# Weights of the first FFN staged as f32 and cast by GpSimd, x^T made on TensorE, weights of the last FFN pre-cast: an 8-core decoder trunk on Trainium2

## Chip, cores, metric

The kernel runs on all 8 cores of one Trainium2 chip (two dies: cores 0 to 3 and 4 to 7). Every core does the same work on two of the 16 sequences, with no traffic between cores. The metric is device microseconds of the slowest core.

Some executions fall in a slow state: the cores of one die or both show a lower granted TensorE clock and the time is some per cent longer. Only fast executions enter a ratio. On the chips of this study the slow state was so frequent (kernel before: 5813 to 6769 us) that I use three measures, and name which one I quote:

- the **ratio** to the kernel before of the same rounds, fast executions only, with its 95% interval;
- the **die difference**: over all executions of a kernel, I take every die whose mean granted clock was above 0.968, average the spans of its four cores, and subtract the same mean for the kernel before on the same chip in the same rounds. "±" is twice the standard error over such dies. Moving the threshold to 0.965 moved the differences by about 2 us, apart from the two slowest kernels, which then count more dies and read 8 to 10 us longer;
- the **delay curve**, from the one profiled (fast) execution: the time at which a given share of all matmul columns has started, averaged over the 8 cores, minus the same of the kernel before. It compares single executions, so its end value carries some ±10 us, but its steps over a short stretch carry much less.

## The reference, cut

```python
D_MODEL, BATCH, SEQ, D_FF = 1024, 16, 2048, 2816
def _swiglu(x, w_gate_up, w_down):
    gate, up = jnp.split(x @ w_gate_up, 2, axis=-1)
    return (jax.nn.silu(gate) * up) @ w_down
# layer 0: half FFN -> HGRN2 gated recurrence -> half FFN -> shared K/V
# layer 1: half FFN -> forgetting attention ("FoX") -> half FFN
for l in range(2):
    x = _layer_norm(alpha * x + 0.5 * _swiglu(x, w_gate_up[l, 0], w_down[l, 0]), ...)
    y = _hgrn2(x, ...) if l == 0 else _fox(x, k, v, c, ...)
    x = _layer_norm(alpha * x + y, ...)
    x = _layer_norm(alpha * x + 0.5 * _swiglu(x, w_gate_up[l, 1], w_down[l, 1]), ...)
    # after layer 0: k, v, c = _shared_kv(x, ...)
```

There are four FFN halves, numbered f = 0 to 3. All weights arrive as f32; the kernel multiplies in bf16.

## The kernel before: the parts that matter

Every operation is first *recorded* with a modelled cost and its dependences. A list scheduler then plays the program through a simple model in time, and the order it finds is what each engine's instruction queue gets. On the chip each engine works through its queue in that order (e1 below shows VectorE stand still behind a waiting instruction). So the model of a DMA transfer decides the order of instructions.

```python
def shared(work, overlap):
    overlap = max(0.0, overlap)
    return 2 * work if overlap >= 2 * work else work + overlap / 2

def list_schedule(ops, key):
    ...
        if o.dma is not None:
            if e == "pool":                              # GpSimd: the software queue
                st = max(t + cost + 1.0, sw_free)
                sw_free = o.end = st + shared(o.nbytes / 135e3, dma_free - st)
                o.end += 1.5
            else:                                        # SyncE: the hardware queue
                st = max(t + cost + 1.0, dma_free)
                dma_free = o.end = st + shared(o.nbytes / 300e3, sw_free - st)
                o.end += 1.0
    ...
```

Weights are cast f32 to bf16 by the DMA itself the first time they are used (this has to be issued from GpSimd: the Trainium skill, "DMA: Bandwidth & Descriptors", section "Rules for kernel authors"; all casting transfers are issued there). The bf16 copy is written back to DRAM, and later uses read it over the hardware queue:

```python
    def wload(self, th, key, dst, bufs, chan, scr, src, nb):
        R = self.R
        wb = self.wsb.get(key)
        if wb is None:
            wb = self.wsb[key] = Buf()
            R.dma("pool", [(dst, src)], reads=[self.gate] if th else [], writes=bufs, chan=chan, nbytes=nb)
            R.dma("sp", [(scr, dst)], reads=bufs, writes=[wb], chan=self.wch.next(), nbytes=nb)
        else:
            R.dma("sp", [(dst, scr)], reads=[wb], writes=bufs, chan=chan, nbytes=nb)
```

The two sequences are cut into 8 blocks of 512 rows, and the stages are recorded in a hand-written order: `p` the first FFN of blocks 0 and 1 together, `a` that of another block alone, `h` HGRN2, `c` the FFN after it, `k` K/V, `d` the third FFN, `x` attention, `e` the last FFN, `i` the load of a block's x^T.

```python
    def record(self):
        ...
        self.xin(0, *blk[0])        # x^T of a block: 1 MB as bf16, by a casting transfer
        self.xin(1, *blk[1])
        ...
        head = "p0 i2 h0 a2 h1 h2 c0 k0 d0 x0 c1 k1 d1 x1 c2 k2 d2 e0 x2 i3 a3 e1 h3 i4 a4"
    ...
    def ffn(self, blocks, f):
        ...
        for half in range(2):
            for jj in range(HJ):
                j = half * HJ + jj
                w = self.wg.next()
                self.wload(0, ("gu", f, j), w.t[:], [w.b], w.b, self.wgu_s[f, j], self.wgu_f[f, j], 1 << 19)
                if jj in (1, 3, 5):
                    ...                                        # one third of this half's w_down
                    self.wload(0, ("dn", f, half, g), ...)
                ...                                            # gate, up, tanh, two multiplies
            for (n, s, b), (hT, hTb, rD, banks, lt) in work:
                ...                                            # down projection, residual, layer norm
```

The softmax here doesn't subtract the row's maximum and nothing guards it: scores larger than these inputs give would overflow.

## Time and profile before

| | before |
|---|---|
| four executions | 5829.5, 5834.3, 5836.6, 6063.0 (slow) us, median 5835.4 |
| cores of the profiled execution | 5777.0 to 5848.9 us, mean 5815.1, mean granted clock 0.972 to 0.977 |
| PE (TensorE) busy, slowest core | 5478.3 us |

In the profile PE is TensorE, PEld its weight loads, DVE VectorE, ACT ScalarE, POOL GpSimd and SP SyncE; a q after a name marks what the engine's sequencer does, such as issuing a transfer. A buffer is written `out<-in`.

Lines of the profile's page of the kernel before. The first gives the span; then PE's busy time (its share of the span and the instructions); then, for 40 equal slices of the span, PE's busy share and the mean of the 16 DMA engines in tenths; last, the chain of waits by engine.

```profile
span 5848.9 us, 77661 instructions; the slowest of 8 cores (5777.0 to 5848.9 us)
...
PE 5478.3 (94%) x31296; PEld 2603.6 (45%) x31296; DVE 3056.6 (52%) x5516; ACT 2129.0 (36%) x4154; POOL 273.8 (5%) x410
...
PE   6988989899997999999999999999999999989998
...
DMA  9678897965669864656566374664656556455454
...
PE 81%; DMA 11%; DVE 3%; ACT 2%; issue 2%; SPq 1%; POOL 0%; DVEq 0%; POOLq 0%; ACTq 0%
```

PE is the limit. What can be gained is its 370 us of idle time, most of it in the first third. The change aims at two stretches: the first slice, and slices 13 and 14 (1755 to 2047 us), where DMA stands at 9 and 8.

What PE waited for in the first 250 us of the kernel before (line, what it waited for: us in total, times, longest):

```profile
core 6 of [0, 1, 2, 3, 4, 5, 6, 7], span 5848.9 us
...
PE pb L650 <- DMA wg_6<-w_gu: 36.7, 2, 25.6
PE pb L650 <- DMA wg_10<-w_gu: 9.0, 1, 9.0
PE pb L650 <- DMA wg_8<-w_gu: 7.6, 2, 6.1
```

And between 1650 and 2020 us, where the last FFN's first pass (`e0`) runs beside an attention block (`x2`):

```profile
core 6 of [0, 1, 2, 3, 4, 5, 6, 7], span 5848.9 us
...
PE pb L1108 <- DMA fka_2_72<-ka_d: 30.1, 3, 22.8
PE pb L1108 <- DMA fka_2_73<-ka_d: 10.0, 1, 10.0
...
```

`fka` are the attention's keys. They come late because f32 weights (`w_gu`, `w_dn` of f = 3) fill the DMA engines. The busy times of both stretches on core 6 (window: its length, then busy us of PE, PEld, DVE, ACT, POOL, the granted clock, DMA share, GB/s):

```profile
0.00:110.00 110.00, 58.12 (x224) 23.91 (x224) 26.02 (x65) 9.85 (x16) 11.46 (x28) 0.86 1.00 214
...
1740.00:1990.00 250.00, 204.21 (x1364) 102.35 (x1363) 85.12 (x149) 90.04 (x179) 19.71 (x34) 0.90 0.85 202
...
```

PE idles 52 us in the first, 46 us in the second. And the DMA queues in the first 250 us (queue: packets, MB, share of the 16 engines' time):

```profile
q0 software_dynamic: 6944, 22.58, 58.5%
q1 hardware_dynamic: 8920, 25.96, 32.0%
...
```

Software transfers took 58.5% of the engines' time for 22.58 MB: 0.585 x 250 / 22.58 = 6.5 us per MB. Hardware ones took 3.1.

### The profile page before, as it was taken

To read this page: it belongs to the slowest core of one execution; us is meant where nothing else is said; L and a number is where in the kernel's file an instruction comes from. 1 tells how busy PE (TensorE), PEld (TensorE's weight loads), DVE (VectorE), ACT (ScalarE), POOL (GpSimd) and SP (SyncE) were. 2 spreads that over 40 slices of the span, in tenths; PEclk is the share of its full clock that TensorE was granted. 3 is DMA by queue.
4 is the path that set the end of the run, shared out by engine and by line. 5 is a ranking of instruction groups with operands and counts; after the bars stand their busy time and mean duration, and the time that the engine had idled before them with its cause. 6 is when DMAs were issued, how large, how long until landed. Compare 5 with 4: busy or idle time off the path is not lost.

```text
span 5848.9 us, 77661 instructions; the slowest of 8 cores (5777.0 to 5848.9 us)
## 1 busy us (share of the span) xinstructions
PE 5478.3 (94%) x31296; PEld 2603.6 (45%) x31296; DVE 3056.6 (52%) x5516; ACT 2129.0 (36%) x4154; POOL 273.8 (5%) x410
## 2 busy tenths in 40 slices
PE   6988989899997999999999999999999999989998
PEld 2443434444543444444454445444454444544544
DVE  2466656554543546667454653556535565244255
ACT  1153535221313315253331525325253351742720
POOL 1001111000000000000000000000000000000000
PEclk8999989999998999999999999999999999999999
DMA  9678897965669864656566374664656556455454
GB/s 216 164 202 219 199 240 178 250 200 177 185 195 214 220 207 131 203 175 211 185 179 213 118 233 159 208 198 140 202 174 196 183 180 204 159 189 187 141 175 155
DMA packets 383494, 1106.28 MB, mean 189 GB/s; under 512 B 66784, under 2 KB 80800, under 8 KB 370592
## 3 DMA queue, kind: packets, MB, share of 16 engines
q1 hardware_dynamic: 353840, 1004.80, 53.8%
q0 software_dynamic: 29296, 96.51, 10.4%
q8 instruction: 248, 4.06, 0.3%
q14 instruction: 110, 0.90, 0.1%
HBM read 989.54 MB, written 208.14 MB: 205 GB/s over the span
## 4 chain that ended last, share of the span: by engine, by line
PE 81%; DMA 11%; DVE 3%; ACT 2%; issue 2%; SPq 1%; POOL 0%; DVEq 0%; POOLq 0%; ACTq 0%
PE pb L650 70%; PE pb L1108 4%; PE pb L1124 2%; DMA ka_d<-hT 2%; DMA lw_38<-hqf_s 1%; DMA wg_9<-wgu_s 1%; PE pb L697 1%; PE pb L961 1%; DMA fka_2_72<-ka_d 1%; DMA wg_6<-w_gu 1%; DMA v_d<-hT 1%; SPq L244 1%; DMA wg_7<-wgu_s 1%; PE pb L940 1%; PE pb L957 1%
## 5 line engine op out<-in xcount | busy, mean ns | idle before, releaser
L650 PE MATMUL pb<-wd,hT 128*128 128x512 bf16 x5456 | 1247.5, 380 | 12.5 <-DVE rD_15 L762 5.3
L650 PEld LDWEIGHTS pb<-wd,hT 128*128 128x128 bf16 x5456 | 523.2, 98 | 613.9 <-DVE hT L738 8.8
L732 ACT ACTIVATE sg_14<-pb 128x512 f32<-128x512 f32 x352 | 210.0, 597 | 920.5 <-PE pb L650 917.7
L732 ACT ACTIVATE sg_13<-pb 128x512 f32<-128x512 f32 x352 | 209.9, 596 | 892.5 <-PE pb L650 891.1
L735 DVE SCALAR_TENSOR_TENSOR sg_14<-sg_14,pb 128x512 f32<-128x512 f32 x352 | 241.3, 685 | 553.9 <-ACT sg_14 L732 553.4
L735 DVE SCALAR_TENSOR_TENSOR sg_13<-sg_13,pb 128x512 f32<-128x512 f32 x352 | 241.2, 685 | 460.7 <-ACT sg_13 L732 459.8
L738 DVE SCALAR_TENSOR_TENSOR hT<-sg_14,pb 128x512 bf16<-128x512 f32 x352 | 241.0, 685 | 175.2 <-PE pb L650 158.1
L738 DVE SCALAR_TENSOR_TENSOR hT<-sg_13,pb 128x512 bf16<-128x512 f32 x330 | 225.7, 684 | 161.1 <-PE pb L650 146.9
L650 PE MATMUL pb<-xT_3,wg_6 128*128 128x512 bf16 x880 | 212.7, 389 | 38.6 <-DMA wg_6<-w_gu 36.7
L650 PE MATMUL pb<-xT_3,wg_10 128*128 128x512 bf16 x880 | 209.8, 387 | 19.8 <-DMA wg_10<-w_gu 9.0
L650 PE MATMUL pb<-xT_3,wg_8 128*128 128x512 bf16 x896 | 214.7, 386 | 14.4 <-DMA wg_8<-w_gu 7.6
L650 PE MATMUL pb<-xT_4,wg_10 128*128 128x512 bf16 x912 | 214.9, 381 | 9.0 <-DVE hT L992 7.1
L650 PE MATMUL pb<-xT_3,wg_7 128*128 128x512 bf16 x880 | 210.0, 385 | 6.0 <-DMA wg_7<-wgu_s 4.1
L650 PE MATMUL pb<-xT_4,wg_9 128*128 128x512 bf16 x848 | 200.4, 382 | 13.9 <-DMA wg_9<-wgu_s 6.4
L650 PE MATMUL pb<-xT_4,wg_6 128*128 128x512 bf16 x912 | 213.3, 382 | 0.0
L650 PE MATMUL pb<-xT_4,wg_8 128*128 128x512 bf16 x880 | 206.4, 381 | 7.1 <-DMA wg_8<-wgu_s 3.5
L650 PE MATMUL pb<-xT_3,wg_9 128*128 128x512 bf16 x880 | 203.9, 379 | 0.3 <-DMA wg_9<-wgu_s 0.2
L650 PE MATMUL pb<-xT_4,wg_7 128*128 128x512 bf16 x864 | 200.9, 379 | 2.4 <-DVE hT L992 1.2
L650 PE MATMUL pb<-xT_5,wg_9 128*128 128x512 bf16 x592 | 141.9, 384 | 13.9 <-DMA wg_9<-wgu_s 10.0
L650 PE MATMUL pb<-xT_5,wg_7 128*128 128x512 bf16 x608 | 146.6, 385 | 6.2 <-DMA wg_7<-wgu_s 3.3
L1117 ACT ACTIVATE fPT_2_76<-pb 128x512 bf16<-128x512 f32 (+1 forms) x216 | 122.9, 569 | 71.0 <-PE pb L1108 44.1
L650 PEld LDWEIGHTS pb<-xT_3,wg_6 128*128 128x128 bf16 x880 | 85.6, 100 | 140.9 <-issue 34.4
(507 smaller groups left out, 9307.5 us busy)
## 6 DMA issues: line engine op xcount, KB each, us to landing
wd<-wdn_s SPq DMA_DIRECT2D x108, 1024.0 KB, 7.4
wg_9<-wgu_s SPq DMA_DIRECT2D x120, 512.0 KB, 4.4
wg_10<-wgu_s SPq DMA_DIRECT2D x120, 512.0 KB, 4.8
wg_8<-wgu_s SPq DMA_DIRECT2D x119, 512.0 KB, 4.8
wg_7<-wgu_s SPq DMA_DIRECT2D x118, 512.0 KB, 4.8
wg_6<-wgu_s SPq DMA_DIRECT2D x117, 512.0 KB, 4.7
wd<-wdn_s SPq DMA_DIRECT2D x54, 768.0 KB, 10.3
wd<-w_dn POOLq DMA_DIRECT2D x16, 1024.0 KB, 14.4
```

Of the source, the lines that this page charges most:

```text
L244: ins = eng.dma_start(out=dst, in_=src)
L650: ins = e.matmul(out, lhsT=pairs[i][0], rhs=pairs[i][1], start=(start and i == 0), stop=(stop and i == n - 1))
L697: ins = e.transpose(qv[:, k, :], xb.t[:, k * 128:(k + 1) * 128], self.ident.t[:])
L732: R.op("act", lambda e, sg=sg, pg=pg: e.activation(out=sg.t[:], in_=pg.t[:], func=AF.Tanh, scale=0.5), reads=[pg.b], writes=[sg.b], cost=c ...
L735: R.op("dve", lambda e, sg=sg, pg=pg: e.scalar_tensor_tensor(out=sg.t[:], in0=sg.t[:], scalar=1.0, in1=pg.t[:], op0=ALU.add, op1=ALU.mult) ...
L738: R.op("dve", lambda e, sg=sg, pu=pu, jj=jj, hT=hT: e.scalar_tensor_tensor(out=hT[:, jj, :], in0=sg.t[:], scalar=0.25, in1=pu.t[:], op0=AL ...
L940: ins = e.matmul(Uv[:, x, :], lhsT=bt.t[:, t, :], rhs=V.t[:, t, hv], start=True, stop=True)
L957: R.op("pe", lambda e, t=t, pov=pov, pt=pt, hv=hv: e.matmul(pov[:, t, :], lhsT=pt.t[:, t, :], rhs=V.t[:, t, hv], start=(t == 0), stop=Fals ...
L961: R.op("pe", lambda e, t=t, cc=cc, c=c, pov=pov, A=A, sp=sp: e.matmul(pov[cc * 64:(cc + 1) * 64, t, :], lhsT=A.t[:, c * 64:(c + 1) * 64], ...
L1108: first = ins = e.matmul(ps.t[:, c0:512], lhsT=ka.t[:, i * 128:(i + 1) * 128], rhs=qa.t[:, h4, c0:512], start=True, stop=(i < 4 * b))
L1117: R.op("act", lambda e, ps=ps, pt=pt, c0=c0: e.activation(out=pt.t[:, c0:512], in_=ps.t[:, c0:512], func=AF.Exp), reads=[ps.b], writes=[pt ...
L1124: ins = e.matmul(accv[:, t, 0:65], lhsT=pt.t[:, t * 128:(t + 1) * 128], rhs=Vt.t[:, i, vo:vo + 65], start=(i == 0 and t == 0), stop=(i == ...
```

## The change

The intent: at the start, take the casting load off the software queue (f32 over the hardware queue into two staging buffers, GpSimd casts), and do not load x^T of the first two blocks but make it on TensorE from x, which is needed anyway. Later, convert the last FFN's weights DRAM to DRAM ahead of need, while other stages run, so that `e0` only loads bf16. With this comes a new DMA model in the scheduler: other rates, and transfers that slow each other on both queues.

The diff, cut to its core:

```diff
-def shared(work, overlap): ...
 def list_schedule(ops, key):
         if o.dma is not None:
-            if e == "pool":
-                st = max(t + cost + 1.0, sw_free)
-                sw_free = o.end = st + shared(o.nbytes / 135e3, dma_free - st)
-                o.end += 1.5
-            else:
-                st = max(t + cost + 1.0, dma_free)
-                dma_free = o.end = st + shared(o.nbytes / 300e3, sw_free - st)
-                o.end += 1.0
+            work = o.nbytes / (140e3 if e == "pool" else 325e3)
+            mine, other = (sw_free, hw_free) if e == "pool" else (hw_free, sw_free)
+            st = max(t + cost + 1.0, mine)
+            both = min(work, max(0.0, other - st))
+            mine, other = st + work + both, other + both
+            sw_free, hw_free = (mine, other) if e == "pool" else (other, mine)
+            o.end = mine + 1.5
...
 def wload(...):
-        if wb is None:
+        if wb is None and self.staged:                  # only the first FFN of blocks 0 and 1
+            ... for d, c in parts:
+                st = self.lw.next()                     # one of two staging buffers, seen as f32
+                R.dma("sp", [(f, c)], writes=[st.b], chan=st.b, nbytes=n * 512)
+                R.op("pool", lambda e, d=d, f=f: e.tensor_copy(out=d, in_=f), reads=[st.b], writes=bufs, ...)
+            R.dma("sp", [(scr, dst)], reads=bufs, writes=[wb], chan=self.wch.next(), nbytes=nb)
+        elif wb is None:
...
+    def precast(self, key, gate):                       # DRAM f32 -> DRAM bf16, all on one channel
+        ...
+        self.R.dma("pool", [(scr, src)], reads=[gate], writes=[wb], chan=self.cch, nbytes=nb * 1.3)
...
 def record(self):
-        self.xin(0, *blk[0])
-        self.xin(1, *blk[1])
+        pre = {"d1": gu(3, 0, 6), "c2": gu(3, 6, 16), "d2": gu(3, 16, 22) + dn(3)}
...
+    def xin_pe(self, n, s, b, rD, banks, lt):           # x -> bf16 (VectorE) -> 8 transposes (PE) -> xT (ScalarE)
...
 def ffn(self, blocks, f):
+                for _ in range(due):                    # pre-casts spread over the steps of d1, c2, d2
+                    key = self.pq.pop(0)
+                    if key: self.precast(key, step[0])
```

"All on one channel" means that every pre-cast waits for the one before it to land.

More of the change, by code (lines that the diff above doesn't have):

```diff
@@ L103, in dma @@
         return o
-def shared(work, overlap):
-    overlap = max(0.0, overlap)
-    return 2 * work if overlap >= 2 * work else work + overlap / 2
 def list_schedule(ops, key):
@@ L124, in list_schedule @@
     avail = {e: [] for e in engs}
-    dma_free = sw_free = 0.0
+    hw_free = sw_free = 0.0
     tset = None
@@ L387, in build @@
         self.gate = Buf()
+        self.cch = Buf()
+        self.staged = False
+        self.pq = []
         self.wch = Ring([Buf() for _ in range(8)])
@@ L591, in wload @@
         wb = self.wsb.get(key)
-        if wb is None:
+        if wb is None and self.staged:
+            wb = self.wsb[key] = Buf()
+            parts = [(dst, src)] if key[0] == "gu" else [(dst[:, k:min(k + 2, dst.shape[1])], src[:, k:min(k + 2, dst.shape[1])])
+                                                         for k in range(0, dst.shape[1], 2)]
+            for d, c in parts:
+                st = self.lw.next()
+                n = int(np.prod(d.shape[1:]))
+                f = st.t[:].bitcast(F32)[:, 0:n]
+                if len(d.shape) == 3:
+                    f = f.rearrange("p (k c) -> p k c", c=d.shape[2])
+                R.dma("sp", [(f, c)], writes=[st.b], chan=st.b, nbytes=n * 512)
+                R.op("pool", lambda e, d=d, f=f: e.tensor_copy(out=d, in_=f), reads=[st.b], writes=bufs,
+                     cost=0.2 + n / 960.0)
+            R.dma("sp", [(scr, dst)], reads=bufs, writes=[wb], chan=self.wch.next(), nbytes=nb)
+        elif wb is None:
             wb = self.wsb[key] = Buf()
@@ L597, in wload @@
             R.dma("sp", [(dst, scr)], reads=[wb], writes=bufs, chan=chan, nbytes=nb)
+    def precast(self, key, gate):
+        if key[0] == "gu":
+            scr, src, nb = self.wgu_s[key[1:]], self.wgu_f[key[1:]], 1 << 19
+        else:
+            f, half, g = key[1:]
+            k0, nk = WD_GROUPS[g]
+            rows = slice((half * HJ + k0) * 128, (half * HJ + k0 + nk) * 128)
+            scr, src, nb = self.wdn_s[f, rows], self.wdn_f[f, rows], nk << 18
+        wb = self.wsb[key] = Buf()
+        self.R.dma("pool", [(scr, src)], reads=[gate], writes=[wb], chan=self.cch, nbytes=nb * 1.3)
     def record(self):
@@ L613, in record @@
         tail = "c6 k6 d6 h7 x6 c7 k7 d7 e5 e6 x7 e7"
+        gu = lambda f, a, b: [("gu", f, j) for j in range(a, b)]
+        dn = lambda f: [("dn", f, half, g) for half in range(2) for g in range(3)]
+        pre = {"d1": gu(3, 0, 6), "c2": gu(3, 6, 16), "d2": gu(3, 16, 22) + dn(3)}
         for tok in (head + " " + rest + " " + tail).split():
@@ L626, in record @@
             elif tok[0] == "p":
+                self.pq = pre.get(tok, [])
                 self.ffn([(m,) + blk[m] for m in (n, n + 1)], 0)
             else:
+                self.pq = pre.get(tok, [])
                 self.ffn([(n,) + blk[n]], names[tok[0]])
@@ L634, in xin, with flip, tr @@
                    nbytes=1 << 20)
+    def xin_pe(self, n, s, b, rD, banks, lt):
+        R = self.R
+        for t in range(4):
+            r, xb, q = rD[t], self.xb[lt].next(), banks.next()
+            R.dma("sp", [(r.t[:], self.x_d[s, (b * 4 + t) * 128:(b * 4 + t + 1) * 128, :])], writes=[r.b], chan=r.b,
+                  nbytes=1 << 19)
+            R.op("dve", lambda e, r=r, xb=xb: e.tensor_copy(out=xb.t[:], in_=r.t[:]), reads=[r.b], writes=[xb.b],
+                 cost=c_dve(1024))
+            self.flip(xb, q, n % 3, t, "act")
+    def flip(self, xb, q, slot, t, eng):
+        R = self.R
+        qv = q.t[:].bitcast(BF16).rearrange("p (k c) -> p k c", k=8)
+        def tr(e):
+            first = None
+            for k in range(8):
+                ins = e.transpose(qv[:, k, :], xb.t[:, k * 128:(k + 1) * 128], self.ident.t[:])
+                first = first or ins
+            return (first, ins)
+        R.op("pe", tr, reads=[xb.b, self.ident.b], writes=[q.b], cost=8 * c_pe(128))
+        dst = self.xT[slot][:, :, t * 128:(t + 1) * 128]
+        if eng == "act":
+            R.op("act", lambda e: e.activation(out=dst, in_=qv, func=AF.Copy), reads=[q.b],
+                 writes=[self.xTb[slot][t]], cost=c_act(1024))
+        else:
+            R.op("dve", lambda e: e.tensor_copy(out=dst, in_=qv), reads=[q.b], writes=[self.xTb[slot][t]],
+                 cost=c_dve(1024, 0, 2))
     def mm(self, th, bank, out, pairs, reads, split=4, start=True, stop=True, extra_w=()):
@@ L689, in layer_norm @@
              cost=c_act(1024))
-        tl_ = tg % 4
-        q = bank_ring.next()
-        qv = q.t[:].bitcast(BF16).rearrange("p (k c) -> p k c", k=8)
-        def tr(e):
-            first = None
-            for k in range(8):
-                ins = e.transpose(qv[:, k, :], xb.t[:, k * 128:(k + 1) * 128], self.ident.t[:])
-                first = first or ins
-            return (first, ins)
-        R.op("pe", tr, reads=[xb.b, self.ident.b], writes=[q.b], cost=8 * c_pe(128))
-        R.op("dve", lambda e: e.tensor_copy(out=self.xT[slot][:, :, tl_ * 128:(tl_ + 1) * 128], in_=qv),
-             reads=[q.b], writes=[self.xTb[slot][tl_]], cost=c_dve(1024, 0, 2))
+        self.flip(xb, bank_ring.next(), slot, tg % 4, "dve")
     def ffn(self, blocks, f):
@@ L711, in ffn @@
                  (self.a["phT"][0].t, self.phTb, self.a["prD"], self.bQK, 1)]
+        npq = list(self.pq)
+        self.staged = len(blocks) > 1
         work = list(zip(blocks, homes[::-1][-len(blocks):]))
+        if self.staged:
+            for (n, s, b), (hT, hTb, rD, banks, lt) in work:
+                self.xin_pe(n, s, b, rD, banks, lt)
         for half in range(2):
@@ L725, in ffn @@
                 wv = w.t[:].rearrange("p (k g c) -> p k g c", k=8, g=2)
+                due = len(npq) * (j + 1) // NJ - len(npq) * j // NJ
+                step = [Buf()] if due else []
                 for (n, s, b), (hT, hTb, rD, banks, lt) in work:
@@ L739, in ffn @@
                         out=hT[:, jj, :], in0=sg.t[:], scalar=0.25, in1=pu.t[:], op0=ALU.mult, op1=ALU.mult),
-                        reads=[sg.b, pu.b], writes=[hTb[jj]] + ([self.gate] if len(blocks) > 1 and j == 15 else []),
+                        reads=[sg.b, pu.b], writes=[hTb[jj]] + step + ([self.gate] if len(blocks) > 1 and j == 15 else []),
                         cost=c_dve(512))
+                for _ in range(due):
+                    key = self.pq.pop(0)
+                    if key:
+                        self.precast(key, step[0])
             for (n, s, b), (hT, hTb, rD, banks, lt) in work:
@@ L745, in ffn @@
                     r = rD[t]
-                    if half == 0:
+                    if half == 0 and not self.staged:
                         rows = slice(tg * 128, (tg + 1) * 128)
@@ L766, in ffn @@
                         self.layer_norm(lt, r, s, tg, n % 3, f == 3, banks)
+        self.staged = False
     def out_proj(self, n, s, b, w_s, w_f, scale):
```

## The prediction

> **What bounds it now.** The matrix engine: PE is busy 5478 of 5849 us (engine table); the chain of waits is 81% PE, 11% DMA. The change can touch two pieces of the 370 idle us.
>
> *Start.* In the stretch table PE works 58 of the first 110 us: 52 idle, DMA engines at 97-108%, PE waiting for `wg<-w_gu` (25.6 us to the first matmul, 28 us more after).
>
> *First pass of the last FFN, beside an attention block (1780-1960 us).* DMA is saturated again while f32 weights come on the software queue; PE idles 45 us, 40 of them waiting for `fka<-ka_d` (once 22.8 us).
>
> **Costs.** By the DMA queues of the first 250 us, software took 58.5% of the engines' time for 22.6 MB landed, hardware 32.0% for 26.0 MB: estimates of 6.5 and 3.1 us per MB. A gate-up weight is 0.52 MB as bf16, so 3.4 us by software; 1.05 MB as f32, so 3.2 us by hardware. Moving the queue saves almost no engine time. That agrees with the Trainium skill, "DMA: Bandwidth & Descriptors", section "Issuing engines are not separate DMA queues". Removed at the start: loading x^T for two blocks: 2 x 1.05 MB x 6.5 = 14 us of DMA time.
>
> Added: 64 transposes (8 took 0.6 us), 8 VectorE casts, 8 ScalarE copies, all before PE has work; 33 GpSimd casts of up to 128x2048. The skill, "GPSIMD Engine Reference", section "Engine selection", calls one-input work roughly line rate; I estimate 2-2.5 us each. But they lie in a latency chain: two staging buffers, each doing load, land, cast, and every reload queues behind a bf16 write-back. All of x (4.2 MB) and the layer-norm rows now precede the first weight.
>
> Hand estimate: first FFN matmul at 30-35 us; then a staged chunk every 4.8-5.5 us. Down weights are interleaved early, so the third, fifth and seventh gate-up tiles come late: 15-25 us of stalls, 0-7 us more after the first down projection. Idle 47-65 us against 52: expected loss 6 us.
>
> Pre-casting: the last FFN's 34.6 MB of f32 are converted DRAM to DRAM, one transfer at a time, in 1100-1750 us (DMA share 0.6-0.75). It adds 112 us of engine time there (17.3 MB x 6.5): share 0.8-0.9. In 1740-1990 us it removes the same 112 us; the bf16 write-back is replaced by a bf16 load. DMA share there falls from 85% to near half. Gain 35 of the 40 us. Cost: 10 us of new attention waits in 1100-1750, or layer norms held up behind a blocked GpSimd queue.
>
> **Sum.** 35 - 10 - 6 = 19 us gained: 5815 us, 80% range 5775-5862. The schedule is recomputed with other DMA rates, so small waits everywhere move: +-15 us. Faster by over 2%: 0.04; within 2%: 0.93; slower by over 2%: 0.03.
>
> **What would show it.** PE idle in the first 110 us still 45-65, first FFN matmul after 28 us, PE waits naming GpSimd casts. Cast mean 2-2.5 us. `fka<-ka_d` waits over 10 us gone from the stretch of the last FFN's first pass, PE idle there under 12 us. DMA share 0.8-0.9 in 1100-1750, with some more idle. PE busy total within 10 us of before.
>
> **What would make it wrong.** Casts at 4 us or more (start loses 20 us); f32 by hardware faster than 3.1 us per MB once software is off the rings (start gains 15); pre-casts blocking GpSimd's in-order queue so that layer norms stall PE for tens of us; the reordering hurting an attention stage.

## The result, and the profile after

| | before | after |
|---|---|---|
| executions, us | 5829.5, 5834.3, 5836.6, 6063.0 (slow) | 5876.7, 5898.1, 5908.3, 6023.9 (slow) |
| median, us | 5835.4 | 5903.2 |
| ratio of fast runs | | 1.0101, 95% interval 1.0064 to 1.0138 |
| mean of the 8 cores in the profile | 5815.1 us | 5864.4 us (+49) |
| mean granted clock of the 8 cores | 0.975 | 0.974 |

The ratio counts a fifth execution of the kernel after as well (5886.0 us, fast). A ratio is the mean time of one kernel's fast runs over that of the other's of the same rounds, so it is not quite the ratio of the medians quoted. The change made the kernel 1% slower. That is inside the 2% which counts as the same, but outside its own noise, and outside the predicted range (5775 to 5862 us).

The page of the kernel after, the same parts:

```profile
span 5897.1 us, 77865 instructions; the slowest of 8 cores (5821.7 to 5897.1 us)
...
PE 5502.8 (93%) x31360; PEld 2613.7 (44%) x31360; DVE 3064.0 (52%) x5524; ACT 2140.4 (36%) x4162; POOL 315.1 (5%) x414
...
PE 81%; DMA 10%; DVE 3%; ACT 3%; issue 1%; SPq 1%; POOL 1%; POOLq 0%; DVEq 0%; ACTq 0%
```

PE's waits in the first 250 us of the kernel after:

```profile
core 1 of [0, 1, 2, 3, 4, 5, 6, 7], span 5897.1 us
...
PE pb L680 <- DVE xbL L668: 20.9, 3, 19.2
PE pb L706 <- POOL wg_8 L599: 16.3, 2, 9.8
PE pb L706 <- POOL wg_7 L599: 4.5, 2, 4.2
PE pb L706 <- POOL wg_10 L599: 4.4, 1, 4.4
...
```

The 19.2 us are the wait for the first block of x (the transposes begin at 19.17 us). After that PE waits for GpSimd's casts. Between 1700 and 2100 us PE's longest wait in the kernel after is now another:

```profile
core 1 of [0, 1, 2, 3, 4, 5, 6, 7], span 5897.1 us
...
PE pb L706 <- DMA wg_7<-wgu_s: 20.1, 2, 15.2
...
```

`wgu_s` are the bf16 weights that the pre-casts write. The load that PE waits for 15.2 us was issued at 1862.55 us, when their last pre-cast had long been issued (1775.38) but those of `w_dn` were still running (the last was issued at 1868.92). The same windows of the kernel after, on its slowest core (core 1):

```profile
0.00:110.00 110.00, 63.66 (x275) 29.11 (x276) 30.03 (x72) 17.31 (x23) 28.06 (x27) 0.89 0.92 270
...
1740.00:1990.00 250.00, 225.97 (x1452) 111.37 (x1451) 89.08 (x151) 87.75 (x176) 8.48 (x15) 0.96 0.75 188
...
```

On these two cores both target stretches got better: PE idles 46 us instead of 52 in the first and 24 instead of 46 in the second. The mean of the 8 cores confirms the second (41.6 us before, 24.8 after) but hardly the first (52.0 and 50.4 in the first 110 us, 57.1 and 58.2 in the first 300). Yet the kernel is slower, so the loss lies elsewhere. The mean PE idle time of the 8 cores, worked out from both traces (us):

| stretch, us | before | after |
|---|---|---|
| 0 to 100 | 51.4 | 45.0 |
| 100 to 300 | 5.7 | 13.2 |
| 600 to 1000 | 46.6 | 77.2 |
| 1400 to 1800 | 21.4 | 35.7 |
| 1800 to 2000 | 38.6 | 21.0 |
| 0 to 5600 | 341 | 369 |

Between 600 and 1000 us 31 us are lost, in a stretch (HGRN2 beside FFN) where the change adds no instruction at all. 28 of the 49 us are idle time; the rest is PE busy time. Of that rest, 8 us are the transposes (8 groups of 1.03 us in the trace); part of the other goes with the lower granted clock (see "PE busy total" below).

What PE waited for from 650 to 1150 us, first in the kernel before (lines of VectorE's products alone):

```profile
core 6 of [0, 1, 2, 3, 4, 5, 6, 7], span 5848.9 us
...
PE pb L650 <- DVE sg_13 L735: 2.5, 2, 1.7
...
PE pb L902 <- DVE hB_2_52 L894: 2.2, 3, 1.2
...
PE pb L650 <- DVE sg_14 L735: 0.8, 1, 0.8
...
```

and in the kernel after:

```profile
core 1 of [0, 1, 2, 3, 4, 5, 6, 7], span 5897.1 us
...
PE pb L958 <- DVE hB_2_52 L950: 13.6, 5, 6.8
...
PE pb L706 <- DVE sg_14 L786: 6.7, 4, 4.3
PE pb L706 <- DVE sg_13 L786: 6.5, 4, 3.7
...
```

`hB` is a product of HGRN2 and `sg` the gate of the FFN; VectorE makes both, and PE waits longer for them.

### The profile page after: what moved, and what is told of

Its sections match the earlier page's. It is cut to its first block, busy times and chain, and to the rows that moved or that the text cites. A ratio compares the mean times of both kernels' runs of the same rounds, so it can differ in the third digit from the quotient of the medians.

```text
span 5897.1 us, 77865 instructions; the slowest of 8 cores (5821.7 to 5897.1 us)
## 1 busy us (share of the span) xinstructions
PE 5502.8 (93%) x31360; PEld 2613.7 (44%) x31360; DVE 3064.0 (52%) x5524; ACT 2140.4 (36%) x4162; POOL 315.1 (5%) x414
## 4 chain that ended last, share of the span: by engine, by line
PE 81%; DMA 10%; DVE 3%; ACT 3%; issue 1%; SPq 1%; POOL 1%; POOLq 0%; DVEq 0%; ACTq 0%
PE pb L706 70%; PE pb L1164 4%; DMA lw_38<-hqf_s 3%; PE pb L1180 2%; DMA wg_8<-wgu_s 1%; PE pb L680 1%; PE pb L1017 1%; DMA ka_d<-hT 1%; DMA wg_10<-wgu_s 1%; SPq L237 1%; PE pb L996 1%; DMA lw_39<-w_dn 1%; PE pb L1013 1%; DMA xr_d<-rL_19 1%; DMA fka_2_72<-ka_d 1%
## 5 line engine op out<-in xcount | busy, mean ns | idle before, releaser
L706 PE MATMUL pb<-xT_3,wg_7 128*128 128x512 bf16 x880 | 213.3, 391 | 28.2 <-DMA wg_7<-wgu_s 20.1
L706 PE MATMUL pb<-xT_3,wg_8 128*128 128x512 bf16 x896 | 213.6, 385 | 20.5 <-POOL wg_8 L599 16.3
L706 PE MATMUL pb<-xT_3,wg_10 128*128 128x512 bf16 x880 | 211.6, 388 | 16.2 <-DVE sg_14 L786 4.8
L706 PE MATMUL pb<-xT_4,wg_10 128*128 128x512 bf16 x912 | 214.6, 381 | 9.7 <-DMA wg_10<-wgu_s 4.7
L706 PE MATMUL pb<-xT_4,wg_6 128*128 128x512 bf16 x912 | 213.2, 380 | 3.6 <-DVE sg_14 L786 2.0
L706 PE MATMUL pb<-xT_3,wg_9 128*128 128x512 bf16 x880 | 210.2, 386 | 4.8 <-DMA wg_9<-wgu_s 4.8
L706 PE MATMUL pb<-xT_3,wg_6 128*128 128x512 bf16 x880 | 207.5, 384 | 7.0 <-DVE sg_13 L786 3.7
L706 PE MATMUL pb<-xT_4,wg_8 128*128 128x512 bf16 x880 | 206.0, 380 | 6.0 <-DMA wg_8<-wgu_s 3.4
L706 PE MATMUL pb<-xT_4,wg_9 128*128 128x512 bf16 x848 | 197.2, 379 | 8.6 <-DMA wg_9<-kk_s 2.1
L706 PE MATMUL pb<-xT_4,wg_7 128*128 128x512 bf16 x864 | 200.9, 379 | 4.0 <-ACT hT L1045 1.8
L706 PE MATMUL pb<-xT_5,wg_7 128*128 128x512 bf16 x608 | 143.9, 379 | 4.8 <-DVE sg_13 L786 2.7
L706 PE MATMUL pb<-xT_5,wg_10 128*128 128x512 bf16 x576 | 136.5, 382 | 9.6 <-ACT hT L1045 7.7
L706 PE MATMUL pb<-xT_5,wg_9 128*128 128x512 bf16 x592 | 141.0, 384 | 4.0 <-DMA wg_9<-wgu_s 1.4
```

What stands on the lines that cost most here:

```text
L706: ins = e.matmul(out, lhsT=pairs[i][0], rhs=pairs[i][1], start=(start and i == 0), stop=(stop and i == n - 1))
```

## The experiments

The questions in order: which part of the change costs the time (e1 to e4)? If it is the scheduler's DMA model, is it the size of its rates, its rule, or chance (e5, e6, e7, e9 to e14, e18)? What are the start and the pre-casts worth by themselves (e2, e3, e8, e15, e16, e17)?

Three theories of the model's cost run through the texts. A1: its nominal rates are too high, so consumers are placed too early. A2: chance; any other order is some tens of us worse than one that was tuned by trial. A3: the model tells the scheduler of later data, so it defers work, and an in-order engine then stands still behind an instruction that waits.

All 18 kernels gave correct results. The delay curve of all, as **steps** from one share of the matmul columns to the next (us against the kernel before, where 10% is reached at 671 us, 16% at 1072, 20% at 1319, 28% at 1772, 32% at 2036, 100% at 5800), with the other two measures:

| kernel | to 10% | 10-16 | 16-20 | 20-28 | 28-32 | 32-100 | die difference | ratio [95%] |
|---|---|---|---|---|---|---|---|---|
| after | +1.3 | **+33.7** | +0.3 | +24.6 | -26.4 | +15.7 | +42 ±17 (*) | 1.0101 [1.0064, 1.0138] |
| e1 new DMA model only | -10.1 | **+39.2** | -7.8 | +0.5 | -6.8 | +8.3 | +30 ±10 | 1.0035 [0.9969, 1.0101] |
| e2 start only | -2.9 | +1.4 | +1.5 | +0.7 | -2.0 | -5.6 | -6 ±8 | 0.9995 [0.9940, 1.0050] |
| e3 pre-cast only | +5.4 | -0.9 | +0.1 | +21.1 | -26.8 | +1.4 | +3 ±12 | 1.0001 [0.9931, 1.0072] |
| e4 start + pre-cast, old model (**) | -0.2 | -1.1 | -2.4 | +26.3 | -28.9 | +2.1 | +2 ±10 | 0.9998 [0.9932, 1.0064] |
| e5 change less pre-cast | -0.5 | **+31.2** | -1.6 | +2.3 | -6.7 | +11.0 | +40 ±11 | 1.0071 [1.0048, 1.0093] |
| e6 change, rates -1.5% | +0.9 | **+37.9** | -11.5 | +18.9 | -25.0 | +14.9 | +48 ±10 | 1.0066 [1.0046, 1.0085] |
| e7 change, rates -20% | +25.8 | +77.4 | +0.1 | +24.6 | -30.4 | +80.6 | +178 (one die) | 1.0338 [1.0261, 1.0416] |
| e8 as e4, pre-casts earlier | -2.8 | -1.1 | +6.6 | +25.0 | -44.2 | -4.6 | +1 ±9 | 0.9984 [0.9959, 1.0010] |
| e9 change, old rule, new rates | +4.7 | -0.6 | -7.5 | +22.9 | -22.8 | +9.4 | +21 ±9 | 1.0021 [0.9971, 1.0070] |
| e10 change, new rule, old rates | -6.6 | **+42.1** | -16.0 | +14.2 | -29.4 | -3.5 | +23 ±9 | 1.0016 [0.9952, 1.0080] |
| e11 change, rates +25% | +1.4 | +10.0 | -1.6 | +28.2 | -18.3 | +113.7 | +130 ±10 | 1.0232 [1.0185, 1.0278] |
| e12 as e8, rates +15% | +2.9 | +7.5 | +9.2 | +31.1 | -44.0 | +61.5 | +63 ±16 | 1.0148 [1.0083, 1.0213] |
| e13 change, half of the rule: own | -2.2 | +4.8 | -4.7 | +28.4 | -24.5 | +12.1 | +19 ±12 | 1.0035 [1.0006, 1.0064] |
| e14 change, half of the rule: other | +7.1 | +14.1 | +2.2 | +26.8 | -29.2 | +7.0 | +26 ±13 | none (too few fast runs) |
| e15 staged weights only | +22.0 | +3.6 | +0.5 | -0.3 | -0.8 | +0.1 | +27 ±12 | not timed in rounds |
| e16 x^T on TensorE only | -22.7 | +3.9 | -2.3 | -0.8 | -1.0 | +11.3 | -13 ±9 | not timed in rounds |
| e17 x^T on TensorE, early pre-casts | -22.4 | +0.6 | +7.9 | +29.4 | -44.7 | +3.6 | -31 ±10 | 0.9954 [0.9918, 0.9990] |
| e18 control: order of before | -3.9 | +1.9 | +1.3 | +1.8 | -3.0 | +1.2 | -2 ±12 | 1.0032 [0.9995, 1.0068] |

(*) cores of the kernel before are on record for only one execution beside this one. (**) the profile of e4 fell in the slow state on die 0; the curve is that of the cores of die 1 against the same cores of before.

"Old model" is the DMA code of the kernel before; all the others have the code of the kernel after, with the edit shown.

### e1: the new DMA model alone

```diff
 (kernel before)
-            if e == "pool": ... shared(o.nbytes / 135e3, dma_free - st) ...
-            else: ... shared(o.nbytes / 300e3, sw_free - st) ...
+            work = o.nbytes / (140e3 if e == "pool" else 325e3)
+            ... the lines of the change, nothing else
```

> The kernel before with only the scheduler's DMA rates of the change (140 and 325 instead of 135 and 300, +1.5 us for both, and sharing that delays both queues). No instruction is added or removed, they are only reordered. Theory A (the reordering by the new rates costs the time, it is what puts the trunk 30 to 40 us behind between 560 and 1120 us): +30 to +50 us against before, with the milestone of the second recurrence's end (h1, 827 us before) at least 20 us late. Rival B (the staged start, which holds the staging buffers and shifts everything, disturbs the recurrence blocks): within +-12 us of before. Rival C (pre-casting costs it): within +-12 us of before.

Measured: the ratio, 1.0035, was too noisy to tell. The die difference is +30 ±10 us, and the curve loses 39 us between 10% and 16% of the columns, the same place as the kernel after. This kernel has exactly the operations of the kernel before; only their order differs. So the model alone is most of the loss.

How an order loses time can be read on core 5. From the timeline of e1 between 1043 and 1074 us (start, duration, engine, line, operation, out<-in, in brackets the idle time before it and what ended that):

```profile
1043.27 0.32 SPq L237 DMA_DIRECT2D rL<-xr_d  x1
...
1071.49 1.41 DVE L797 SCALAR_TENSOR_TENSOR rL<-rL,pb 128x512 f32<-128x512 f32 x2 [18.96 <-DMA rL<-xr_d]
1072.82 0.68 DVE L728 SCALAR_TENSOR_TENSOR sg<-sg,pb 128x512 f32<-128x512 f32 x1
...
1073.56 2.74 PE L643 MATMUL pb<-xT,wg 128*128 128x512 bf16 x6 [16.57 <-DVE sg L728]
...
```

The residual rows `rL` are asked for at 1043.27 us, among f32 weight loads, and let VectorE go on only at 1071.49. VectorE had nothing else wrong: its next instruction, L728 of the FFN, was ready, but stands behind L797 in the queue. PE needs L728 and idles 16.57 us.

This wait is not what the kernel after suffers from, though. Worked out from the traces for 600 to 1150 us (mean of the 8 cores): the idle time of PE that VectorE ended is 30 us before, 35 in e9 (below) and 48 to 58 in the five kernels with the whole rule at nearly these rates (after, e1, e5, e6, e10). Of it, VectorE stood waiting for `rL` for 6 us before and 16 in e1 and e6, but for only about 2 in after, e5 and e10. In the kernel after VectorE was at work on other instructions in 38 of the 50 us (before: 20 of 30). So what the five share is that PE waits longer for VectorE; the late transfer is one way to it.

### e2, e3, e4: the other parts, with the old model

```diff
 (kernel after, with the DMA code of before)
 e2: -        pre = {"d1": gu(3, 0, 6), "c2": gu(3, 6, 16), "d2": gu(3, 16, 22) + dn(3)}
     +        pre = {}
 e3: -        self.staged = len(blocks) > 1
     +        self.staged = False              # and xin(0), xin(1) back in record()
 e4: both parts as in the change
```

> The kernel before with only the staged first FFN and x^T by TensorE; old scheduler rates, no pre-casting. Theory A: -5 to +10 us against before (the start gains what the trace showed, about 4 to 6 us idle less in the first 100 us and as much more up to 260). Rival B: +25 to +45 us, with h1 and h2 20 us or more late.

> The kernel before with only the pre-casting of the last FFN's weights; old rates, old start. Theory A, and my prediction's sum for this part: -10 to -30 us against before (the stretch 1780 to 2000 us gains about 35, 1100 to 1750 loses 10 to 20). Rival C: 0 to +30 us, because the pre-casts cost as much in 1100 to 1860 us as they give back.

> The whole change but with the scheduler's old DMA rates. Theory A: 20 to 40 us faster than the changed kernel with the new rates (5903), so 5800 to 5840, below the kernel before by up to 30. Rivals B and C: within 15 us of the changed kernel, 5880 to 5915.

Measured: die differences of -6 ±8, +3 ±12 and +2 ±10 us. None of the three has a step between 10% and 16%. So the start and the pre-casts together are worth nothing, and nothing is lost by them either; a gain of 19 us is excluded by e4. In e3 the pre-casts cost 21 us between 20% and 28% (1319 to 1772 us) and give back 27 us in the next stretch.

What runs into the second stretch shows on GpSimd's queue. From the timeline of GpSimd on core 4 of e3 (the operation here is the *issue* of a transfer):

```profile
1577.08 0.57 POOL L244 DMA_DIRECT2D wgu_s<-w_gu  x1 [10.45 <-DMA wgu_s<-w_gu]
1594.04 0.52 POOL L244 DMA_DIRECT2D wgu_s<-w_gu  x1 [16.39 <-DMA wgu_s<-w_gu]
1605.31 0.52 POOL L244 DMA_DIRECT2D wgu_s<-w_gu  x1 [10.75 <-DMA wgu_s<-w_gu]
...
1778.66 0.58 POOL L244 DMA_DIRECT2D wdn_s<-w_dn  x1 [17.58 <-DMA wdn_s<-w_dn]
...
1819.78 0.64 POOL L244 DMA_DIRECT2D wdn_s<-w_dn  x1 [17.37 <-DMA wdn_s<-w_dn]
```

Each of these waits for the one before; such issues follow it by 7 to 19 us. They are 11 of the 28; 14 others wait for the FFN step that releases them (`DVE hT` in `prof e3_precast_only --core 4 --waits --engine POOL`). The pre-casts start at 1331 us here and run past 1800, into the stretch that they were meant to free. I had assumed 1100 to 1750.

### e5, e6, e7: the change without pre-casts; its rates a little and much lower

```diff
 e5: -        pre = {"d1": ...}              e6: -  140e3 ... 325e3     e7: -  140e3 ... 325e3
     +        pre = {}                           +  138e3 ... 320e3         +  112e3 ... 260e3
```

> The changed kernel without pre-casting: staged start and new rates. Theory A (order, by the new rates, is the loss; it lies before 1120 us and has nothing to do with pre-casting): +30 to +45 us late at 20% of the matmul columns and about as much at the end, so 5860 to 5880, and the stretch 1800 to 2000 us again idles 35 to 40 us. Rival (pre-casting costs it): within 10 us of the kernel before.

> The changed kernel with the scheduler's rates 138 and 320 in place of 140 and 325. Reading A1 (the new rates are systematically too high): within 10 us of the changed kernel (mean of cores +39 to +59 us against before), since 1.5% is next to nothing. Reading A2 (a list schedule of this length is chaotic; any change of its inputs moves the first 1100 us by tens of us): a mean of cores that differs from the changed kernel's by 15 us or more, either way.

> The changed kernel with rates 112 and 260, a fifth lower. Reading A1 (too high rates put instructions ahead of data that isn't there yet): the loss between 10% and 16% of the columns shrinks from 35 us to under 15, and the kernel is 20 to 40 us faster than the changed one. Reading A2: anything from -45 to +30 us, without relation to the rates.

Measured: e5 is at +40 ±11, with the step of 31 us between 10% and 16%. Against e1 it adds the start, which changes nothing within the noise.

e6 is the test of chance. A change of 1.5% does reshuffle the order: by the traces of core 1, only about 70% of VectorE's instructions between 620 and 1130 us stand in the same relative order as in the kernel after. If A2 were right the loss should scatter; it came out at +48 ±10 with the step of 38 us at the same place. That speaks against A2, but it is one more order, not many (see e9).

e7 is the test of A1: with rates 20% lower data is modelled as later, and the loss should shrink. It grew to +178 us. A1 falls.

### e8: pre-casts that end before `e0`

```diff
 (as e4)
-        pre = {"d1": gu(3, 0, 6), "c2": gu(3, 6, 16), "d2": gu(3, 16, 22) + dn(3)}
+        pre = {"c1": gu(3, 0, 4), "d1": gu(3, 4, 14), "c2": gu(3, 14, 22), "d2": dn(3) + [None] * 6}
```

> The whole change with the scheduler's old rates, and the pre-casts begun one FFN earlier (c1) and ended half way through d2, so that none is still running when the last FFN begins. If the tail of the pre-casts, running past 1800 us into the last FFN's first pass, is what kept 20 us idle there: idle of 1800 to 2000 us falls from 20 to under 12 us, the loss up to the end of d2 stays 15 to 30 us, and the mean of cores ends 10 to 25 us before the kernel before. If contention beside the attention blocks is the cost wherever the pre-casts lie: within 8 us of the kernel before.

Measured: the mean idle time of the 8 cores between 1800 and 2000 us falls to 6.0 us (38.6 before, 20.9 in e3), and the step from 28% to 32% is -44 instead of -27. So the late pre-casts were what remained there. PE's longest waits between 1700 and 2020 us in e8 no longer name a pre-cast's transfer first:

```profile
core 4 of [0, 1, 2, 3, 4, 5, 6, 7], span 5819.3 us
...
PE pb L713 <- DVE hT L796: 12.4, 4, 7.4
...
PE pb L713 <- DMA wg<-wgu_s: 4.2, 1, 4.2
```

The whole time does not confirm the gain: the profiled execution's cores average 21 us less than those of before, but over all executions the die difference is +1 ±9 against +2 ±10 for e4. I count the local effect as shown, and a gain in time from e8 alone as not shown.

### e9, e10, e11, e12: rates and rule apart; higher rates

```diff
 e9:  -            both = min(work, max(0.0, other - st))
      -            mine, other = st + work + both, other + both
      +            mine = st + shared(work, other - st)
 e10: -  140e3 ... 325e3      e11: -  140e3 ... 325e3     e12 (as e8): -  135e3 ... 300e3
      +  135e3 ... 300e3           +  175e3 ... 406e3                  +  155e3 ... 345e3
```

> The changed kernel with the scheduler's new rates (140 and 325, +1.5 us) but the old rule for two queues at once: the later transfer alone is lengthened, by half of the overlap, and the other queue isn't delayed. Run 7 fell out against my reading of too high rates: a fifth lower made it 128 us worse. New reading A3: what hurts is that the new rule tells the scheduler of later data, so it defers the work that waits for it on the in-order engines, and PE runs out of ready work. A3 expects the loss between 10% and 16% of the matmul columns gone (under 10 us instead of 35) and a mean of cores within 12 us of run 4 on the undisturbed die (-4 us against before). Reading A2 (chaos): anything between -20 and +50 us, no relation to the rule.

> The changed kernel with the old rates (135 and 300) but the new rule, which delays both queues. A3: worse than the changed kernel or equal to it, since data is told later still: +45 to +90 us against before in the mean of cores. A2: -20 to +50 us. If the new rates and not the rule were to blame: within 12 us of run 4.

> The changed kernel with the new rule and rates 175 and 406, a quarter higher. A3: data is told earlier, so most of the loss goes: -15 to +15 us against before in the mean of cores, and under 15 us of loss between 10% and 16% of the columns. A2: no relation, -20 to +50. If higher rates put work ahead of its data: +60 us or more.

> Run 8 (old rule, staged start, early pre-casts) with rates 155 and 345, 15% higher than the old ones. A3: equal or better than run 8, which was 21 us before the kernel before in the mean of cores: -20 to -35 us. If the old rates already were about right, 0 to -15 us. Also the try at a version that beats both kernels.

Measured: with the old rule there is no step between 10% and 16%, at the new rates (e9) as at the old; with the new rule at the old rates (e10) there is one of 42 us. **The local loss goes with the rule.** The traces set a limit to this. I compared VectorE's order from 620 to 1130 us on core 1: eight of the ten kernels with the old rule keep the order of the kernel before there, so their missing step says nothing of other orders. Only e9 and e12 reorder it (74% and 85% of the instructions in the same relative order); their steps are -1 and +8 us. After and e5 share one order; those of e1, e6 and e10 resemble each other (76 to 84%). And the whole rule at rates 25% higher (e11) loses only 10 us. So the rule costs this at rates near its own, in two families of orders; with so few, chance is unlikely rather than excluded. In e10 a part is given back by 20% and 32%, as in e1 and e6.

The rates cost later. From 32% on, the seven kernels with 140/325 or 138/320 lose 7 to 16 us (after, e1, e5, e6, e9, e13, e14; mean 11), the eight with 135/300 (not counting the control e18) between -6 and +11 (mean 0.6; seven of them within ±6). Higher rates lose steadily more there: 62 us at +15% (e12) and 114 at +25% (e11); but so do lower ones, 81 us at -20% (e7). So A3 in the plain form "tell the scheduler of earlier data and it gets better" fails for rates: the order is best near the old rates, and worse on both sides. A3's numbers were missed too: it had expected +45 to +90 for e10, -15 to +15 for e11 and -20 to -35 for e12. e12 was meant as the best version; it is 63 us slower than the kernel before.

By die differences, with both parts of the change in: old model +2 ±10 (e4), new rates alone +21 ±9 (e9), new rule alone +23 ±9 (e10), both +42 ±17 (after) and +48 ±10 (e6). The two add up. One detail is not separated: e9 and e10 both have the hardware queue's landing time of 1.5 us instead of 1.0.

### e13, e14: the two halves of the rule

The new rule does two things when transfers overlap: it lengthens the transfer being placed by the whole overlap, and it pushes back the other queue.

```diff
 e13: -            mine, other = st + work + both, other + both
      +            mine = st + work + both                          # own only; the other queue is left
 e14: +            mine, other = st + shared(work, other - st), other + both   # other only; own as before
```

> The changed kernel, but of the new two-queue rule only the first half: a transfer that meets one on the other queue is lengthened by up to its own work (the old rule: by half of the overlap), the other queue isn't delayed. In the stretch from 10% to 16% of the matmul columns all four kernels with the whole new rule at rates near 140 and 325 lost 30 to 45 us, all with the old rule under 8. If this half does it: a loss of 25 to 45 us there; if the other half does it: under 10 us.

> The changed kernel with only the second half of the new rule: the other queue's next transfer is delayed by the overlap; a transfer's own length is by the old rule. If this half does it: a loss of 25 to 45 us between 10% and 16% of the columns; if the first half does it: under 10 us. If both runs show under 10 or both over 25, it is not one half of the rule.

Measured: between 10% and 16%, +5 us for the own half and +14 for the other half; the whole rule has 31 to 42. Delaying the other queue is the larger half, but neither makes the loss alone, and by whole time they cannot be told apart (+19 ±12, +26 ±13, where new rates with the old rule have +21). Nor should more be read into 5 against 14 us: e13's order is nearly that of e9 in this stretch (92%), so it hardly tests its half, and e11 and e12 lose 8 to 10 us there without either half alone.

### e15, e16: the two parts of the start

```diff
 (as e2)
 e15: weights staged and cast by GpSimd, x^T loaded as before:
 -            self.xin_pe(...)            +  self.xin(0, *blk[0]); self.xin(1, *blk[1])
 e16: x^T on TensorE, weights as before:
 -        if wb is None and self.staged:
 +        if wb is None and False:
```

> The kernel before with only the staged weights (f32 by hardware, GpSimd casts); x^T of the first two blocks still by the software queue, old rule and rates, no pre-casting. My prediction held that moving the queue saves almost no engine time and that the gain at the start is the x^T transfers: then the idle of the first 300 us is 5 to 20 us more than with x^T by TensorE (run 2: about 57 us, kernel before 57) so 60 to 78, and the first FFN matmul comes at 28 to 36 us. If staging itself is the gain: 57 us or less.

> The kernel before with only x^T of the first two blocks by TensorE; weights still cast by the software queue, old rule and rates, no pre-casting. By my prediction's account (14 us of DMA time saved): the idle of the first 300 us is 5 to 14 us less than before, so 43 to 52 us. If x^T by TensorE only moves the wait (all of x before the first matmul): 55 us or more.

Measured (one look each): by 10% of the columns e15 is 22.0 us behind and e16 22.7 ahead. The idle time of PE in the first 300 us is 75.5 us in e15 and 45.9 in e16, against 57.1 before. Both fall where the texts above put them if the prediction's account held (60 to 78 and 43 to 52). So the start of the change is the sum of a gain and a loss: of the same size by the curve, 11 and 18 us by the idle time of the first 300 us. PE's waits of the first 250 us, first e15:

```profile
core 5 of [0, 1, 2, 3, 4, 5, 6, 7], span 5873.7 us
...
PE pb L715 <- POOL wg L606: 71.9, 6, 33.1
...
```

and e16:

```profile
core 1 of [0, 1, 2, 3, 4, 5, 6, 7], span 5839.2 us
...
PE pb L687 <- DVE xbL L675: 26.2, 3, 21.0
PE pb L687 <- DVE xbD L675: 10.9, 2, 8.4
PE pb L713 <- DMA wg<-w_gu: 4.8, 1, 4.8
...
```

In e16 the first FFN matmul comes late (42.9 us, against 25.6 before), but then the weights keep up. In e15 PE waits for casts again and again. The casts themselves are short; from the timeline of GpSimd in the kernel after:

```profile
34.03 1.89 POOL L599 CAST wg_6<-lw_38 128x2048 bf16<-128x2048 f32 x1 [26.93 <-DMA lw_38<-w_gu]
37.06 1.89 POOL L599 CAST wg_7<-lw_39 128x2048 bf16<-128x2048 f32 x1 [1.15 <-DMA lw_39<-w_gu]
51.41 1.89 POOL L599 CAST wd<-lw_38 128x2048 bf16<-128x2048 f32 x1 [12.45 <-DMA lw_38<-w_dn]
```

A cast takes 1.89 us, and GpSimd waited 12.45 us for the landing of what it casts. It is the chain "buffer free, load, land, cast" over two buffers that PE waits for, not GpSimd's speed.

### e17 and e18: the parts that gain, and a control

```diff
 e17: as e8, and  -  if wb is None and self.staged:   +  if wb is None and False:
 e18: kernel after with the old model, pre = {}, staged = False, xin(0) and xin(1) back
```

> What the runs favour, put together: x^T of the first two blocks by TensorE (run 16: 20 us ahead at 20% of the columns), the first FFN's weights on the software queue as before, pre-casts begun in c1 and ended half way through d2 (run 8 gained about 18 us over run 4 by it), the scheduler's old rule and rates. If the parts add up: 30 to 45 us before the kernel before in the mean of cores, ratio 0.992 to 0.996. If the gains overlap or the new order costs something elsewhere: 10 to 25 us.

> Control: the changed source with every part switched off and the old rule, whose instruction order on every engine is that of the kernel before. It shows how much of a difference of the curves (the time at which a share of the matmul columns has started, mean of cores) is chance: within 6 us of the kernel before everywhere, ratio 0.998 to 1.002.

Measured: e18 has the same order of instructions as the kernel before. Its curve stays within 4 us of it, its die difference is -2 ±12, and its ratio is 1.0032. So a ratio of ±0.3% on such a chip is noise, and several of the ratios above (e1, e9, e10, e13) show nothing by themselves.

e17 (x^T on TensorE, weights cast by the DMA, early pre-casts, old model) is the fastest kernel: ratio 0.9954 [0.9918, 0.9990], die difference -31 ±10 us. It beats the kernel before in the same rounds, and by these measures the kernel after too, which did not run in them. Its profiled cores average 5789.5 us, 26 us less than before's. I had expected 30 to 45, and the two measures lie on either side of its lower end: in the curve the gain of x^T (22 us by 10%) and that of the pre-casts (-45 after +29) do not quite add up, because 8 us go between 16% and 20%.

## Why the prediction was wrong, point by point

**The step that failed** is this one, in the prediction's words: "The schedule is recomputed with other DMA rates, so small waits everywhere move: +-15 us." I took the new order as noise around zero, of at most 15 us. It is a systematic loss of 40 to 46 us (after or e6 against e4, +42 ±17 or +48 ±10 against +2 ±10). By whole time about half goes with the new rule (+23 ±9 in e10): it is lost in one place, between 10% and 16% of the columns (31 to 42 us in all five kernels with the whole rule at nearly these rates, at most 8 in all ten with the old rule, eight of which kept the old order there), and in part given back later. About half goes with the rates (+21 ±9 in e9); the curves place some 11 us of it in the later two thirds, the rest is not placed. The sum in the prediction's terms: order +40 to +46 instead of 0, pre-casts about 0 instead of -25, start about 0 instead of +6. The same sentence even names the rates and overlooks the rule, which is the larger edit in that function. "The reordering hurting an attention stage" was among the things that would make it wrong; it hurt HGRN2 beside FFN instead. What is not settled is why the rule does it. PE's idle time that VectorE ends grows there from 30 us before to 50 after (600 to 1150 us); the in-order wait of 19 us for a transfer that e1's trace shows is a part of this in e1 and e6, and not in the kernel after.

**"Gain 35 of the 40 us", then "Cost: 10 us".** The kind was right, the cost term mis-sized. The `fka` waits are gone, and the stretch gives back 26 us in the kernel after (27 in e3, 29 in e4). The cost before it is 21 to 26 us, not 10. The net is nothing instead of +25. Two reasons show: the DMA share in 1200 to 1600 us rose only from 0.64 to 0.69, not to 0.8 to 0.9, because the pre-casts began at 1385 us and not at 1100, held back by the FFN steps that release them and by each other; and so the share in 1600 to 1800 us went from 0.70 to 0.86, and the last was issued at 1868.92 us. The predicted "PE idle there under 12 us" was 21.0 us (24 on the core shown, over 1740 to 1990 us); e8 got it to 6.0 by starting earlier.

**The start, "expected loss 6 us".** Measured -6 ±8 (e2): close to nothing. "Moving the queue saves almost no engine time" held: per MB landed as bf16, two MB of f32 at 3.1 us replace one at 6.5. That the engines are shared between the queues, as the Trainium skill says ("DMA: Bandwidth & Descriptors", section "Issuing engines are not separate DMA queues"), agrees with the DMA share of 0.92 that the first 110 us still have after the move (1.00 before). The net came near by two terms of opposite sign: I had put "14 us of DMA time" for x^T and 15 to 25 us of stalls for the chain. By the curve x^T gains about 23 us (e16) and the chain costs about 22 (e15); by PE's idle time of the first 300 us it is 11 and 18. First FFN matmul at 36 us (35.97, just outside the predicted 30 to 35), idle time of the first 110 us 46 us on the slowest core (50.4 in the mean; predicted 45 to 65), PE waits naming casts: as predicted.

**Casts "2-2.5 us each".** 1.89 us, so 2048 / 1.89 = 1080 elements per us and partition. "Roughly line rate" in the Trainium skill ("GPSIMD Engine Reference", section "Engine selection") fits, if it is read loosely: VectorE's cast of 128x1024 took 0.69 us in the same trace, 1480 elements per us and partition, so GpSimd had 73% of its rate.

**"PE busy total within 10 us".** It rose by 24.5 us between the two slowest cores (5478.3 to 5502.8); 8 us of it are the transposes. The two cores also differ in granted clock, 0.974 and 0.971; among the cores of the kernel before PE's busy time went from 5457 us at 0.977 to 5483 at 0.973. If it goes as one over the clock, the difference is worth some 17 us (an estimate from these figures). Nothing tests that.

**The chances.** "Within 2%", given 0.93, holds. The sign and the range did not: +1% instead of -0.3%.

## What to carry to other kernels

Where a scheduler with a cost model decides the instruction order, a change of that model is a change of the kernel: run it alone first. Here kernels whose modelled DMA rates were moved by 15% up, 25% up or 20% down ran 63 to 178 us longer than before, and the new model alone cost 30 us although no operation changed. A chain of transfers has to be costed by when each may start (here 7 to 19 us after the one before, or with the step that releases it) and not by the engine time it uses alone, and it has to end before the stretch that it is meant to free. Split a change into its parts before adding up a sum: at the start of this one, a gain was hidden by a loss of about its size.

## What the Trainium skill lacked or had wrong

- "GPSIMD Engine Reference" has no measured time for a dtype-converting copy: f32 to bf16 took 1.89 us for 128x2048.
- "DMA: Bandwidth & Descriptors" says that a cast during a DMA must be issued from GpSimd, but not what it costs: in the first 250 us, casting software transfers together took 6.5 us of all 16 engines' time per MB landed, and hardware transfers 3.1.
- The same page has no figure for casting transfers from DRAM to DRAM: one at a time, beside other traffic, an issue that waited for the landing of the one before came 7 to 19 us after it (e3; 0.5 to 1 MB of bf16 each).
- "TensorE: Matmul & The Clock Gate", part 1, section "Seeing it yourself", says that a die goes to 13/16 of the clock within 5 to 20 us of a third core starting dense matmuls, and stays there while the load lasts. Here PE was busy for 93 to 94% of each slowest core's span, at a mean granted clock of 0.97 to 0.98 in fast executions. Only the dies of slow executions came near 13/16 in the mean (0.813 to 0.816 on the four cores of one die in a run of e12, 6700 us), others lay between (0.85, 0.91). This need not contradict the page, for the traces have no common time for the cores: in the slow die of e4's profile, cores 0 and 1 were granted 13/16 only from 42 to 1026 us of their spans and cores 2 and 3 only from 5077 us to their ends, which would fit two pairs of cores that ran at the same time for only so long. Whether they did, and so why a die falls into that state, none of the runs shows.
- No page puts a number on what a late transfer costs the work queued behind it that does not need it: in e1 VectorE stood still for 18.96 us and PE for 16.57. In the mean of the cores such waits for `rL` made up 16 us of PE's idle time between 600 and 1150 us in e1, and 2.5 in the kernel after.
